# Loads of the scan's factors and stores of its inverses issued by SyncE instead of GpSimd

## The chip, the cores and the metric

The kernel runs on one core of a Trainium2 chip. Engines are named as in the profile: PE (TensorE matmul), PEld (its weight load), DVE (VectorE), ACT (ScalarE), POOL (GpSimd) and SP (SyncE, which computes nothing here and only issues transfers). "SPq", "ACTq" and "POOLq" are rows in which an engine issues a transfer. The metric is the device time of one execution in microseconds (us), as the median of the runs shown.

## What is computed

The reference is the trunk of a diffusion backbone with two layers over 1024 latent tokens and 256 context tokens of width 1024. Layer 0 mixes with pooling and neighbourhood attention, layer 1 with a bidirectional RWKV-7 recurrence; each is followed by a squared-ReLU MLP. The change lies in the recurrence of layer 1:

```
def step(S, inp):
    w_t, k_t, v_t, kk_t, kka_t = inp[:5]
    S = (S * w_t[:, :, None, :]
         - jnp.einsum('bhij,bhj->bhi', S, kk_t)[..., None] * kka_t[:, :, None, :]
         + v_t[..., None] * k_t[:, :, None, :])
    y = jnp.einsum('bhij,bhj->bhi', S, inp[5]) if emit else None
    return S, y
...
for d, reverse in enumerate((False, True)):
    s_ctx, y_c = wkv_scan(s0, decay_c, k_dc, v_c, kk_c, a_c, r_c, reverse)
    _, y_d = wkv_scan(s_ctx, decay, k_d, v, kk, a, r, reverse)
```

16 heads of 64 carry a state of 64 x 64 each, forward and in reverse; the context's final state starts the latent scan.

## The kernel before

All arithmetic is fp32, as products of fp32 matmuls or of split operands. The program runs in stages: layer 0, its MLP, the features of layer 1 (`l1_features`), the scan (`l1_scan`), the readout (`l1_readout`) and the second MLP.

The features stage leaves in DRAM, for each chunk of 64 tokens and each direction, the factors of the scan (`ft`, loaded into tiles `FT`), the strictly lower score blocks (`ls`) and the values (`v1scr`). The scan works through 20 steps, 4 of context (s = 0 to 3) and 16 latent ones (s = 4 to 19), each with two halves, one for each direction d. What a half needs:

- `FT` (L1574, function `load`): the factors of step s and direction d, in one of four fixed tiles, loaded by quarters (two head pairs each) of 256 KB, or 192 KB in the context. The first step's loads are issued by ACT, all others by Pool. `scores` (L1626, tile `sc`) read them one quarter at a time, `stack` (L1608) copies a part, `readout_state` (L1701) reads another part.
- `D` (L1578, `load_values`): the values, on SP.
- `G` and `ZT` (L1594, L1595, `load_blocks`) and `TT` (L1603, `load_inverses`): blocks of `ls` and of the inverses, in many 128-byte rows, on SP. `compose1` (L1653) and `compose2` (L1667) join two 32-row inverses into a 64-row one.
- `chain_x`, `chain_u`, `chain_s` (L1678, L1686, L1729) carry the state `SS` on; `readout_values` (L1713) ends in the copy `yt` (L1717) on ACT and two stores `yscr` (L1720) on SP.

The 32-row inverses come from `scan_blocks` and `scan_invert`. For two steps at a time, eight loads fill `M` from `ls` (L1497, on SP), Pool sets `X` to the identity (L1501, L1502), and DVE does 31 rank-one updates (`tmp` L1511, `X` L1515), then a transposed copy (L1518). `X` and `M` are stored to DRAM as `lt` and `ltt` (L1522, L1523), from which `TT` and `ZT` of two steps are loaded. Ten such blocks are needed. The two first are inverted during the features stage; the other eight run on DVE in the background of the scan, one update at each call of `fill()`, which stands eight times in each half. Early readout work takes their place once they are done.

From step 0 on the order of instructions is the order in which the code is written (`manual_schedule`), engine by engine. In half d of step s stand, in this order among others: the values of step s + 1; `chain_x`; scores of the first quarter of s + 1; quarters 2 and 3 of an FT tile loaded half a step after its quarters 0 and 1; `chain_u`; blocks or `compose1`; `readout_state` and `chain_s`; quarter 0 of FT for step s + 2; `readout_values`; inverses or blocks for s + 2; the last scores; quarter 1 of FT for s + 2. So every quarter is asked for at least half a step before its scores run.

An engine issues its transfers in order, and a transfer that waits holds up all behind it. SP and ACT transfers complete on eight semaphores taken in turn (DMAHW0 to DMAHW7 in the order's rows), Pool's on eight others (DMASW0 to DMASW7); before a transfer is issued, the one that had its semaphore before must have landed. So SP and ACT together have at most eight transfers in flight, and Pool eight more.

Of the kernel before, what the change touches and what calls it, by code (L numbers as in the profile page):

```python
# [58 lines left out]
class Trunk:  # L59
# [1445 lines left out]
    def scan_invert(self, ip, b, M, X):  # L1505

        nc = self.nc
        for c in range(31):
            m, n = c + 1, 31 - c
            tmp = ip.tile([128, 256], F32, tag="tmp", name="tmp", bufs=1)[:, :m * n].rearrange("p (a b) -> p a b", a=m)  # L1510
            nc.vector.tensor_tensor(  # L1511
                out=tmp, in0=X[:, 0:m, c:c + 1].to_broadcast([128, m, n]),
                in1=M[:, c:c + 1, c + 1:32].to_broadcast([128, m, n]), op=ALU.mult,
            )
            nc.vector.tensor_tensor(out=X[:, 0:m, c + 1:32], in0=X[:, 0:m, c + 1:32], in1=tmp, op=ALU.subtract)  # L1515
            yield
        XT = M
        nc.vector.tensor_copy(out=XT, in_=X.rearrange("p r t -> p t r"))  # L1518
        lt = self.scan_dram.tile([128, 32, 32], F32, name=f"lt{b}")
        ltt = self.scan_dram.tile([128, 32, 32], F32, name=f"ltt{b}")  # L1520
        q = nc.sync if b < 2 else nc.gpsimd
        q.dma_start(out=lt, in_=X)  # L1522
        q.dma_start(out=ltt, in_=XT)  # L1523
        self.lt_[b], self.ltt_[b] = lt, ltt

    def l1_scan(self):
        nc, a = self.nc, self.a
        with ExitStack() as es:
# [35 lines left out]
            def load(s, d, parts=range(4)):  # L1564

                if s >= NSTEP:
                    return
                w = W[s]
                F = w["F"][d] = FTs[(2 * s + d) % 4]
                f0 = 0 if w["lat"] else 1  # L1570
                for i in parts:
                    w["got"].add((d, i))
                    hs = slice(2 * i, 2 * i + 2)
                    (nc.scalar if s == 0 else nc.gpsimd).dma_start(out=F[:, hs, 1 + f0:], in_=self.ft[s, d, :, hs, f0:])  # L1574

            def load_values(s, d):
                D_ = hp_.tile([128, 8, 2, CH], F32, tag=f"D{d}", name="D")
# [212 lines left out]
            for d in range(2):  # L1790
                load(0, d)
                load_values(0, d)
                nc.gpsimd.memset(W[0]["D"][d][0:64], 0.0)
# [3 lines left out]
            for d in range(2):  # L1797
                for g in range(4):
                    scores(0, d, g)
                stack(0, d)  # L1800
                load(1, d)
# [10 lines left out]
            for s in range(NSTEP - 1):  # L1812
# [5 lines left out]
                for d in range(2):  # L1818
                    load_values(n, d)
                    chain_x(s, d)  # L1820
                    carry()
                    scores(n, d, 0)
                    load(*later[d], (2,))
                    fill()
                    scores(n, d, 1)
# [31 lines left out]
            s = NSTEP - 1  # L1857
# [392 lines left out]
```

## Time and profile before

| what | us |
|---|---|
| three runs, median (lowest to highest) | 3535.57 (3532.26 to 3536.0) |
| the profiled execution: its own time | 3529.58 |
| the profiled execution: span, first to last instruction | 3527.5 |
| PE busy | 3289.8 (93%) |
| DVE busy | 2049.0 (58%) |
| ACT busy | 1440.4 (41%) |
| POOL busy | 430.9 (12%) |

The span and the 2.1 us around it are the profiled execution's own time. In the table of its DMA queues, q1 is SP's queue (321.55 MB in 405376 packets, 30.9% of the 16 engines' time), q0 is Pool's (81.81 MB in 24640 packets, 7.5%), q10 ACT's (1.77 MB) and q8 and q14 carry instructions. Of the transfers that Pool issues, 152 are FT loads, 8 are lt and 8 ltt stores. The scan lies between about 2190 and 2645 us.

In the lists of waits a row names engine and line, what released it, and the total, the count and the longest wait in us; "issue" as a releaser means that the engine waited for nothing that the profile shows. Timeline rows give start, length, engine, line, operation, output<-input and count, and in brackets the idle time before and its releaser.

### The profile page before, as it was taken

What the parts mean: (1) busy time and instruction counts of PE and PEld (TensorE: products, weight loads), DVE (VectorE), ACT (ScalarE), POOL (GpSimd) and SP (SyncE); (2) the same over time, 40 slices, a digit from 0 to 9 for tenths busy, and PEclk for the clock granted to TensorE, in tenths of its full rate; (3) what the DMA queues carried; (4) which work ended last, traced back from release to release, by engine and by line L of the source; (5) the groups of instructions that cost most, each with busy time, mean ns of one, the idle gap of its engine ahead of it and who ended that gap; (6) DMA issues with size and microseconds to landing.
All of it is one profiled execution on the core that took longest, in us unless ns stands there. A gap on an engine that the chain in (4) does not pass through costs nothing. (4 is left out here: it accounts for less than half of the span.)

```text
span 3527.5 us, 62517 instructions
## 1 busy us (share of the span) xinstructions
PE 3289.8 (93%) x25466; PEld 2747.2 (78%) x25466; DVE 2049.0 (58%) x3903; ACT 1440.4 (41%) x2743; POOL 430.9 (12%) x564
## 2 busy tenths in 40 slices
PE   8999889999999999989988876888888899999998
PEld 4787767888888889867877775777787788888887
DVE  4255555344444354496758988788766734444446
ACT  4244456312121212176758665666664521111112
POOL 0010110000000000023420001232341200000000
PEclk9999999999999999999999898899899899999999
DMA  8433243222222211143227677888873411111112
GB/s 280 149 92 87 91 138 126 96 84 84 75 83 83 78 48 43 36 144 98 77 70 208 213 227 240 174 205 193 224 203 124 156 43 48 48 48 48 48 48 78
DMA packets 432622, 409.11 MB, mean 116 GB/s; under 512 B 151584, under 2 KB 362400, under 8 KB 432336
## 3 DMA queue, kind: packets, MB, share of 16 engines
q1 hardware_dynamic: 405376, 321.55, 30.9%
q0 software_dynamic: 24640, 81.81, 7.5%
q8 instruction: 200, 3.28, 0.4%
q10 hardware_dynamic: 2320, 1.77, 0.2%
q14 instruction: 86, 0.70, 0.1%
HBM read 292.54 MB, written 112.49 MB: 115 GB/s over the span
## 5 line engine op out<-in xcount | busy, mean ns | idle before, releaser
L916 DVE TENSOR_TENSOR yacc<-yps,yacc 128x512 f32<-128x512 f32 x540 | 369.8, 690 | 304.1 <-PE yps L93 303.7
L74 ACT CAST wh<-st 128x1024 fp32r<-128x1024 f32 x160 | 165.0, 1049 | 760.0 <-PE yps L93 557.8
L93 PE MATMUL yps<-wh,xh 128*128 128x512 f32 x1152 | 453.2, 393 | 2.6 <-ACT xh L74 1.5
L93 PE MATMUL yps<-wh,xl 128*128 128x512 f32 x1152 | 448.6, 390 | 0.7 <-DVE xl L75 0.7
L93 PE MATMUL yps<-wl,xh 128*128 128x512 f32 x1152 | 448.9, 390 | 0.0
L75 DVE TENSOR_TENSOR wl<-st,wh 128x1024 fp32r<-128x1024 f32 x160 | 194.3, 1229 | 277.3 <-ACT wh L74 277.1
L93 PE MATMUL acc<-h2h,wh 128*128 128x426 f32 (+3 forms) x768 | 275.6, 359 | 3.1 <-ACT y L671 3.1
L93 PE MATMUL acc<-h2h,wl 128*128 128x426 f32 (+3 forms) x768 | 274.2, 357 | 0.0
L93 PE MATMUL acc<-h2l,wh 128*128 128x426 f32 (+3 forms) x768 | 273.9, 357 | 0.0
L93 PEld LDWEIGHTS yps<-wh,xh 128*128 128x128 f32 x1152 | 216.3, 188 | 70.6 <-DVE yacc L916 11.6
L93 PEld LDWEIGHTS yps<-wh,xl 128*128 128x128 f32 x1152 | 216.1, 188 | 47.8 <-DVE xl L75 2.3
L93 PEld LDWEIGHTS yps<-wl,xh 128*128 128x128 f32 x1152 | 216.3, 188 | 44.8 <-issue 1.7
L898 DVE TENSOR_TENSOR r<-r 128x428 f32<-128x428 f32 (+4 forms) x164 | 102.4, 624 | 243.9 <-ACT r L897 243.8
L93 PE MATMUL acc<-mh,wh 128*128 128x256 f32 (+1 forms) x640 | 215.3, 338 | 4.3 <-ACT mh L74 4.2
L93 PE MATMUL acc<-ml,wh 128*128 128x256 f32 (+1 forms) x640 | 214.4, 335 | 0.0
L93 PE MATMUL acc<-mh,wl 128*128 128x256 f32 (+1 forms) x640 | 214.0, 335 | 0.0
L93 PE MATMUL acc<-h2bh,wh 128*128 128x512 f32 (+3 forms) x544 | 211.9, 389 | 1.4 <-ACT wh L74 0.7
L93 PE MATMUL acc<-h2bl,wh 128*128 128x512 f32 (+3 forms) x544 | 211.8, 389 | 0.8 <-DVE h2bl L288 0.7
L93 PE MATMUL acc<-h2bh,wl 128*128 128x512 f32 (+3 forms) x544 | 211.5, 389 | 0.3 <-DVE wl L75 0.3
L897 ACT ACTIVATE r<-acc 128x428 f32<-128x428 f32 (+4 forms) x164 | 89.2, 544 | 295.1 <-PE acc L93 270.3
L1626 PE MATMUL sc<-FT 64*128 64x192 f32 (+1 forms) x1280 | 144.3, 357 | 16.6 <-issue 6.5
L93 PEld LDWEIGHTS acc<-h2h,wh 128*128 128x128 f32 x768 | 145.0, 189 | 16.1 <-issue 5.1
(322 smaller groups left out, 6996.1 us busy)
## 6 DMA issues: line engine op xcount, KB each, us to landing
st<-in_mlp_w SPq DMA_DIRECT2D x128, 512.0 KB
ft<-F SPq DMA_DIRECT2D x64, 512.0 KB
FT<-ft POOLq DMA_DIRECT2D x128, 256.0 KB, 6.0
adas<-in_ada_w POOLq DMA_DIRECT2D x112, 256.0 KB, 3.8
adas<-in_ada_w SPq DMA_DIRECT2D x80, 256.0 KB
x<-x SPq DMA_DIRECT2D x28, 512.0 KB
bias<-in_bias SPq DMA_DIRECT2D x64, 192.0 KB
ls<-ls SPq DMA_DIRECT2D x80, 128.0 KB
```

Source lines behind the costliest of these rows:

```text
L74: self.nc.scalar.copy(out=hi, in_=src)
L75: self.nc.vector.tensor_tensor(out=lo, in0=src, in1=hi.bitcast(F32), op=ALU.subtract)
L93: self.nc.tensor.matmul(out=ps, lhsT=lhs[x], rhs=rhs[y], start=first and i == 0, stop=last and i == 2)
L897: nc.scalar.activation(out=r, in_=ps, func=AF.Relu)
L898: nc.vector.tensor_tensor(out=r, in0=r, in1=r, op=ALU.mult)
L916: nc.vector.tensor_tensor(out=yacc[t][:, n], in0=ps, in1=yacc[t][:, n], op=ALU.add)
L1626: nc.tensor.matmul(out=p4[:, j, e, f], lhsT=F[st[e], 2 * g + j, 3:5].rearrange("p a t -> p (a t)"), rhs=F[st[e], 2 * g + j, f], start=True ...
```

## The change

Two lines choose another issuing engine. The stores of the inverses b = 2 to 9 (b = 0 and 1 were on SP already) and the loads of the factors for all steps but the first go from `nc.gpsimd` to `nc.sync`. No tile, size or wait condition is written differently.

```
@@ scan_invert
-        q = nc.sync if b < 2 else nc.gpsimd
+        q = nc.sync
         q.dma_start(out=lt, in_=X)
         q.dma_start(out=ltt, in_=XT)
@@ l1_scan, load
-                    (nc.scalar if s == 0 else nc.gpsimd).dma_start(out=F[:, hs, 1 + f0:], in_=self.ft[s, d, :, hs, f0:])
+                    (nc.scalar if s == 0 else nc.sync).dma_start(out=F[:, hs, 1 + f0:], in_=self.ft[s, d, :, hs, f0:])
```

The order of PE, DVE and ACT stays as it was; SP's and Pool's change. On SP at the start of the scan (FT_19564 and FT_19565 are the tiles of step 1, TT_19568 that of step 0) a piece of the difference reads:

```order
 L1595 DMA ZT<-ltt_17783 32x16x32
 L1603 DMA TT_19568<-lt_17782 32x16x32 x2
+L1574 DMA FT_19564<-ft 128x2x192 x4
+L1574 DMA FT_19565<-ft 128x2x192 x4
 L1594 DMA G<-ls 32x16x32
 L1595 DMA ZT<-ltt_17783 32x16x32
```

Eight FT loads, which Pool issued at its own time, now stand behind the last TT of step 0; after them come G, ZT and TT of step 1 (eight loads) and then the eight loads of M for block 2.

On SP in a latent step, with the semaphores that each transfer waits for, the order before is:

```order
L1594 DMA G<-ls 32x16x32 [waits DMAHW7_49,PE_49]
L1595 DMA ZT<-ltt_22925 32x16x32 [waits DMAHW0_49]
L1720 DMA yscr<-yt 64x512 [waits DMAHW1_49,Activation_49]
L1720 DMA yscr<-yt 64x512 [waits DMAHW2_49]
L1594 DMA G<-ls 32x16x32 [waits DMAHW3_49]
L1595 DMA ZT<-ltt_22925 32x16x32 [waits DMAHW4_49]
L1578 DMA D<-v1scr 64x1024 [waits DMAHW5_49]
L1720 DMA yscr<-yt 64x512 [waits DMAHW6_49,Activation_49]
```

From the same G up to the same second pair of yscr, which follows, it now reads:

```order
L1594 DMA G<-ls 32x16x32 [waits DMAHW3_49,PE_49]
L1595 DMA ZT<-ltt_22925 32x16x32 [waits DMAHW4_49]
L1574 DMA FT_19562<-ft 128x2x256 [waits DMAHW5_49,PE_49]
L1720 DMA yscr<-yt 64x512 [waits DMAHW6_49,Activation_49]
L1720 DMA yscr<-yt 64x512 [waits DMAHW7_49]
L1594 DMA G<-ls 32x16x32 [waits DMAHW0_49]
L1595 DMA ZT<-ltt_22925 32x16x32 [waits DMAHW1_49]
L1574 DMA FT_19562<-ft 128x2x256 [waits DMAHW2_49,PE_49]
L1578 DMA D<-v1scr 64x1024 [waits DMAHW3_49]
L1574 DMA FT_19562<-ft 128x2x256 [waits DMAHW4_49,PE_49]
L1574 DMA FT_19562<-ft 128x2x256 [waits DMAHW5_49,PE_49]
L1574 DMA FT_19563<-ft 128x2x256 [waits DMAHW6_49,PE_49]
```

Five FT loads have come in between, each with a wait for PE and in the same turn of eight semaphores as the rest. Pool's order in the scan keeps its memsets and its four early readout products and no transfer but the two D of step 0.

## The prediction

> **What bounds the kernel now.** The page gives the size of the whole and the two data queues. The change touches the scan alone, so I cut its two halves out with the view by stretches.
>
> ```profile
> span 3527.5 us, 62517 instructions
> 2190.00:2314.00 124.00, 100.15 (x2230) 88.59 (x2228) 94.04 (x240) 72.07 (x143) 38.25 (x54) 0.84 0.84 185
> 2314.00:2640.00 326.00, 291.90 (x7238) 259.67 (x7233) 258.91 (x538) 211.82 (x401) 117.40 (x136) 0.94 0.82 208
> ```
>
> The columns are length, busy time of PE, weight load, DVE, ACT and POOL, granted clock, DMA share and GB/s. The scan takes about 450 of 3527.5 us. The 16 DMA engines are busy 82 to 84% of it, and in the long second half PE is busy 291.90 of 326 us, so only 34.1 us of PE idle time are there to be won. What fills them is in the list of PE's waits for that stretch (line, releaser: us in total, times, longest), with PE's share of the scan by steps in the groups of lines:
>
> ```profile
> PE p L1667 <- issue: 6.8, 5, 2.4
> PE yp L1701 <- issue: 4.8, 3, 2.8
> PE sc L1626 <- issue: 4.3, 4, 1.9
> PE yp L1713 <- issue: 2.3, 2, 2.2
> PE xp L1678 <- issue: 1.9, 2, 1.6
> PE p L1653 <- issue: 1.8, 2, 0.9
> PE sp L1729 <- issue: 1.4, 2, 0.9
> PE p L1667 <- DVE SS L1734: 3.4, 3, 1.3
> L1678 PE MATMUL xp<-D,ZQ 128*64 128x64 f32 x928 | 37.1, 238 | 4.6 <-ACT TM L1632 2.7 <-issue 1.9
> ```
>
> No row names a transfer, and the biggest sum, 6.8 + 4.8 + 4.3 + 2.3 + 1.9 + 1.8 + 1.4 = 23.3 us, waits for nothing that the profile shows. 928 matmuls at 64 a step are 14.5 steps in 326 us, 22.5 us a step. The timeline of PE shows where such a gap lies:
>
> ```profile
> 2369.97 1.15 PE L1678 MATMUL xp<-D,ZQ 128*64 128x64 f32 x32 [0.56 <-ACT TM L1632]
> 2371.06 1.57 PE L1626 MATMUL sc<-FT 64*128 64x192 f32 x16
> 2375.83 1.02 PE L1701 MATMUL yp<-SS,FT 64*64 64x64 f32 x26
> 2379.70 0.39 PE L1701 MATMUL yp<-SS,FT 64*64 64x64 f32 x6 [2.84 <-issue]
> 2386.22 0.63 PE L1667 MATMUL p<-TT,G 32*32 32x32 f32 x15 [2.36 <-issue]
> 2386.78 1.98 PE L1678 MATMUL xp<-D,ZQ 128*64 128x64 f32 x32
> 2388.68 2.93 PE L1626 MATMUL sc<-FT 64*128 64x192 f32 x16
> ```
>
> The gap of 2.84 us cuts a group of 32 equal matmuls after the 26th: its inputs were there, so what was late is PE's own instruction stream. After the second gap of 2.36 us the same groups take 1.98 and 2.93 us where they took 1.15 and 1.57: the granted clock has dropped, another 2.2 us. That stream comes by DMA (queue q8 below), over the same engines as the scan's data.
>
> ```profile
> q1 hardware_dynamic: 102952, 36.91, 43.5%
> q0 software_dynamic: 12672, 42.35, 37.2%
> q8 instruction: 67, 1.10, 1.3%
> ```
>
> This is the stretch 2250 to 2640: packets, MB, share of 16 engines. SP's queue q1 moves many small packets (36.91 MB in 102952), Pool's q0 few big ones (42.35 MB in 12672, 3.3 KB each). The change makes q0 empty and gives its bytes to q1.
>
> The first half of the scan is bound otherwise. The chain that ended last runs there through stores of ls, then SP issuing M one by one, then a landing, then DVE without a pause:
>
> ```profile
> 2171.78 9.38 DMA ls<-ls
> 2184.89 3.29 DMA ls<-ls
> 2189.28 6.29 DMA ls<-ls
> 2203.38 1.37 SPq L1497
> 2211.94 1.97 SPq L1497
> 2213.95 2.89 DMA M<-ls
> 2216.96 0.20 DVE tmp L1511
> DVE tmp L1511 <- DMA M<-ls: 6.8, 1, 6.8
> ```
>
> The last row, from the list of waits, is DVE's price for that landing: 6.8 us in which its whole queue stood, the scan's masked copies included.
>
> **The change, part by part.**
>
> *Pool gives up 152 loads of FT and 16 stores of inverses.* Pool's waits in the scan are long, but behind them stands little:
>
> ```profile
> POOL FT L1574 <- ACT TM L1632: 80.7, 12, 13.5
> POOL lt L1522 <- DVE X L1515: 59.4, 6, 18.4
> L1574 POOL DMA_DIRECT2D FT<-ft x152: 724/724/747, 2167.0 to 2624.5; - x152
> L1574 ACTq DMA_DIRECT2D FT<-ft x8: 366/404/1268, 2166.6 to 2180.6; - x8
> PEld sc L1626: 0.3, 1
> DMA to landing us min/median/max: 3.4/6.1/10.0
> ```
>
> Pool saves 152 x 0.724 = 110 us of issuing, worth nothing: Pool is busy 117.40 of 326 us and nobody waits on it in steady state. SP pays about what ACT paid for the same load, 0.40 us. Of the consumers of FT only one matmul waited, 0.3 us: landing after 6.1 us is early enough, since each quarter is asked for at least half a step (11 us) ahead of its scores.
>
> *SP's queue gets them.* A step had on SP 2 D, 2 G, 2 ZT, 4 TT, 4 yscr and, on average, 4 M: 18 issues. It now has 8 FT and one of lt or ltt more: 27, or 0.83 us each in a step of 22.5 us. What one costs on SP now:
>
> ```profile
> 2203.38 11.05 SPq L1497 DMA_DIRECT2D M<-ls  x8
> 2420.20 7.40 SPq L1497 DMA_DIRECT2D M<-ls  x8
> 2431.13 2.17 SPq L1603 DMA_DIRECT2D TT<-lt  x4
> SPq L1720 <- ACT yt L1717: 110.7, 24, 10.4
> ```
>
> Alone, 2.17 / 4 = 0.54 us. In a crowd 7.40 / 8 = 0.93 or 11.05 / 8 = 1.38 us: each waits for the completion of the transfer eight places ahead (the order of SP above), and that one shares the engines with Pool's packets. With Pool silent I take 0.54 to 0.6, the TT row, so 27 x 0.57 = 15.4 us of the 22.5. SP's slack today is 110.7 us of waiting for yt over 16 steps, 6.9 a step, and 15.4 + 6.9 = 22.3 just fits. **Steady issue: 0 us**, covered by that slack and by the half step of lead; if the cover is gone, the price is rival two.
>
> *Waits that SP now takes over.* An FT load waits for the scores, the stack copy or the state readout that free its quarter, an lt store for the end of a DVE inversion (up to 18.4 us, 59.4 in six). Behind them on SP stand TT, D, G, ZT and yscr. They stand behind because the program wrote them later; each is wanted half a step or a step later, and in steady state SP stops at the yt of the same half step anyway. 0 us, with a bound of a few us in the first four steps, where no yscr paces SP.
>
> *The start of the scan.* Before it, ACT and Pool load FT together while the last features are stored:
>
> ```profile
> 2168.53 4.33 POOL L1574 DMA_DIRECT2D FT<-ft  x6
> 2173.49 7.44 ACTq L1574 DMA_DIRECT2D FT<-ft  x4
> 2199.80 5.08 POOL L1574 DMA_DIRECT2D FT<-ft  x7 [7.65 <-ACT ZQ L1608]
> DMA packets 14229, 11.63 MB, mean 291 GB/s; under 512 B 4883, under 2 KB 13459, under 8 KB 14227
> ```
>
> The last row is for 2160 to 2200, when the engines ran full at 291 GB/s. Pool's eight loads there (two, then the six shown) carry 8 x 192 KB = 1.6 MB, and 1.6 MB / 291 GB/s = 5.4 us. They leave this crowd and now stand on SP behind TT, when the ls stores are done: the ls part of the chain (9.38 + 3.29 + 6.29) shortens by up to 5.4. They come ahead of M and push it back by the same 5.4, or by 8 x 0.54 = 4.3. But the seven Pool loads at 2199.80 (1.4 MB, 4.7 us), which ran against M, go behind M in the one queue. M's eight issues fall from 11.05 to 8 x 0.54 = 4.3 at best, 6.7 less; DVE's wait for them is 6.8. So between -5.4 - 6.7 + 4.3 = -7.8 and, if neither crowd clears, +4.3. I take **-6 us**, near the end that the 6.8 us row points to.
>
> *The instruction stream.* With one queue of eight transfers in flight instead of two, a block of instructions should stand behind less. No row shows one queue at this load, so bounds: nothing, or all of 23.3 us plus the slow clock after the longer gaps. The 0.94 of the second half is 0.06 x 326 = 19.6 us of clock; I let half of it hang on these gaps, so -33 at most. A gain beyond zero is what the even spread of gaps while both queues are busy suggests, but the engines stay about as full, since the bytes are the same: I take a quarter of 23.3, **-6 us**. An excess the other way, from SP's packets now coming without pauses, is bounded by the same quarter, +6.
>
> The Trainium skill, page "Runtime: NRT & Kernel Launch", section "Instruction fetch mechanics", says that an engine fetches its program in 16 KiB blocks over its own DMA queue while it runs the last one, and that this is mostly hidden. The gap inside a group of 32 does not agree with "hidden"; by the page this term would be 0 and the time 3529.6 us.
>
> **Sum.** -6 - 6 = -12 us on the profiled execution's 3529.58 us, 3517.6. That execution lies 6.0 us under the median 3535.57 of the three runs, so against the median: **3523.5 us**, its own range 3514 to 3534.
>
> **Rivals.**
>
> *One: nothing moves.* FT was never waited for (0.3 us), so its path is off the chain; at the start the eight loads ahead of M take back what the crowd gives (-5.4 + 5.4); the stream's gaps depend on how full the engines are, which stays. For it: the 0.3 us row and the equal bytes. Against it: the 6.8 us wait of DVE under M's slow issues. 3535.6 us, within 5.
>
> The Trainium skill, "DMA: Bandwidth & Descriptors", section "Issuing engines are not separate DMA queues", gives this rival its rule: the transfers share the same 16 engines whoever issues them, and a second issuer saves only issue time. The small wait on FT agrees with it.
>
> *Two, slower: SP's one queue sets the pace.* Place: any step of the second half; mechanism: 27 issues in order, each waiting for the one eight ahead. It decides from 0.83 us an issue. If they cost what M does at 2420.20, 0.93 us, a step is 27 x 0.93 = 25.1 us, 2.6 more, and 14.5 steps are +38 us: 3573 us; half of it in the steps with M only, 3554. For it: 0.93 and 1.38 are measured, and SP would have no slack over its 6.9 us. Against it: those two were taken against Pool's big packets, which then are gone.
>
> *Three: most of the stream's gaps close.* -6 at the start and -24 of the 33 above: 3505.6 us. For it: the gaps are there only where both queues run. Against it: the engines stay full.
>
> *The change does less than it says* cannot be: SP's order holds all the loads and stores, Pool's none.
>
> **From these to the numbers.** Forecast 0.45, rival one 0.24, two 0.16, three 0.15. A measurement of this kernel tells about 0.2%, 7.1 us, from no change. Faster by more: 0.45 x 0.85 + 0.15 + 0.01 = 0.54; slower by more: 0.16 + 0.02 = 0.18; the rest, 0.28, within. The range reaches from 3503, with rival three in it, to 3550, with the weaker half of rival two; stronger cases of both are left out.
>
> **What would show it.** In the changed profile: q0 nearly empty in the scan and q1 with 1 KB packets in its place; DVE's wait for M under 2 us and the first tmp near 2209 instead of 2216.96; SP's M in groups of eight under 6 us; FT still waited for under 2 us by PE; the sum of "issue" on PE in the second half near 17 us. The prediction is wrong if PE or ACT wait for FT, D or TT by more than 5 us in all (rival two), if M lands no earlier, or if the sum of "issue" grows.

## The result, and the profile after

| | median, us | lowest to highest |
|---|---|---|
| before, six runs beside those of the change | 3533.4 | 3523.63 to 3536.0 |
| the change, six runs | 3512.73 | 3506.29 to 3518.65 |

The ratio is 0.9944, with a 95% interval of 0.9932 to 0.9957: about 20 us less (15 to 24). A second set of six runs of the same changed kernel gave 3512.31 us and a ratio of 0.9956 (0.9943 to 0.9969). In the profiled execution the span is 3504.5 us where it was 3527.5; it was the fastest of its six (3506.29 us), so it shows a little more than the medians.

To see where the time went, all traces are cut at the same four matmuls of PE: the one that stood at 2150 us in the trace of before, and those at 2190, 2314 and 2641.6. The view by stretches then reads, first for before and then for the changed kernel (columns as in the prediction):

```profile
2150.00:2190.00 40.00, 22.21 (x241) 20.00 (x241) 36.71 (x94) 17.44 (x40) 10.03 (x16) 0.71 0.86 270
2314.00:2641.60 327.60, 291.94 (x7239) 259.70 (x7234) 258.91 (x538) 213.34 (x404) 117.40 (x136) 0.94 0.82 209
```

```profile
2145.20:2181.10 35.90, 22.51 (x242) 20.02 (x243) 35.15 (x94) 17.25 (x40) 4.44 (x9) 0.74 0.80 244
2181.10:2307.70 126.60, 101.40 (x2231) 89.39 (x2229) 96.36 (x241) 71.88 (x143) 5.79 (x9) 0.83 0.88 192
2307.70:2620.30 312.60, 285.96 (x7239) 254.54 (x7232) 253.63 (x539) 213.50 (x404) 32.52 (x20) 0.96 0.87 222
```

The end of the features stage gives 40.0 - 35.9 = 4.1 us. The first half of the scan takes them partly back: 126.6 us against 124.0, 2.6 more. The second half is the gain: 312.6 us against 327.6, 15.0 less, of which 6.0 are a shorter busy time of the same matmuls (granted clock 0.96 against 0.94) and 9.0 shorter idle time. The stretch before the scan starts 4.8 us earlier than in before; that comes from stages that the change doesn't touch, and was 1.7 us between the second profiles of the two kernels.

A second profile of each kernel confirms the second half: 326.7 us before (its row stands with the experiments), and for the changed kernel

```profile
2310.40:2624.40 314.00, 284.34 (x7242) 252.89 (x7235) 254.74 (x539) 213.83 (x404) 33.58 (x20) 0.97 0.88 219
```

This is 12.7 us less, of which 3.1 are busy time and 9.6 idle time. So the shorter idle time comes back, and the busy time only by half. Over all three stretches the first pair of profiles gives 491.6 - 475.1 = 16.5 us and the second pair 13.5. The profiles don't place what the medians gain beyond that; single executions of one kernel differ by 12 us (3523.63 to 3536.0).

Pool's queue q0 has lost its load over the whole program and is missing from the second half of the scan, where SP's queue now carries everything:

```profile
q1 hardware_dynamic: 449024, 368.22, 36.0%
q0 software_dynamic: 10560, 35.14, 2.9%
q1 hardware_dynamic: 114788, 68.23, 85.5%
q8 instruction: 57, 0.93, 1.3%
```

The two last rows are those of the second half. What PE waits for there, in the list of waits (line, releaser: us, times, longest):

```profile
PE p L1667 <- DVE SS L1734: 7.6, 5, 2.4
PE p L1667 <- issue: 4.8, 5, 1.5
PE xp L1678 <- ACT TM L1632: 3.1, 4, 1.1
PE up L1686 <- issue: 2.3, 2, 1.5
PE p L1653 <- issue: 2.0, 2, 1.1
PE sc L1626 <- DMA FT<-ft: 1.7, 1, 1.7
PE xp L1678 <- issue: 1.1, 2, 0.8
PE yp L1701 <- issue: 1.1, 2, 0.7
PE sc L1626 <- issue: 0.2, 1, 0.2
```

"issue" is down from 23.3 to 4.8 + 2.3 + 2.0 + 1.1 + 1.1 + 0.2 = 11.5 us, and its longest gap from 2.8 to 1.5 us. DVE's row has grown from 3.4 to 7.6 us, some of the gain given back: PE, early, finds the state `SS` not yet ready (5.8 and 8.3 us in the second profiles). FT is waited for once, 1.7 us. In PE's timeline a gap inside a group of equal matmuls is still there, but short, and the clock stays up behind it (1.15 us for the 32 of `sp`):

```profile
2399.38 0.97 PE L1701 MATMUL yp<-SS,FT 64*64 64x64 f32 x25
2401.04 0.45 PE L1701 MATMUL yp<-SS,FT 64*64 64x64 f32 x7 [0.69 <-issue]
2401.42 1.15 PE L1729 MATMUL sp<-D,TM 128*64 128x64 f32 x32
```

Where such gaps lie can be found by counting PE's instructions in the trace (matmuls, weight loads and those of its sequencer). In before, 18 of the 20 "issue" gaps of the second half lie whole multiples of 256 instructions apart, to within one, and each of the 18 ends 1.3 to 1.7 us after a packet of the instruction queue q8 landed. In the changed kernel it is 13 of 14, 1.2 to 1.9 us after a packet, and in all fourteen profiles of this document together 181 of 207. This shows that PE stands there for the next block of its own program. The blocks are not carried more slowly in before: both kernels have 57 packets of q8 in this half, 16 KB each, and one takes 1.17 and 1.11 us on average in the two profiles of before, 1.14 and 1.20 us in those of the change. What changes is how often a block comes too late.

At the start of the scan the timelines show the ls stores, FT and M on SP, PE's scores of step 0, and DVE's first update:

```profile
2188.38 0.80 SPq L1402 DMA_DIRECT2D ls<-ls  x2
2190.89 4.12 SPq L1574 DMA_DIRECT2D FT<-ft  x8
2201.23 5.27 SPq L1497 DMA_DIRECT2D M<-ls  x8
2188.41 6.19 PE L1626 MATMUL sc<-FT 64*128 64x128 f32 x56 [4.39 <-ACT ls L1400]
2209.69 0.19 DVE L1511 TENSOR_TENSOR tmp<-X,M 128x31 f32<-128x31 f32 x1 [6.84 <-DMA M<-ls]
```

M's eight issues take 5.27 us, where they took 11.05. Yet DVE waits for M as long as before, 6.84 us (in the second profiles 4.7 us before and 7.0 us after). SP's slack, in the list of SP's waits over the whole scan, has shrunk from 110.7 us in 24 waits to:

```profile
SPq L1720 <- ACT yt L1717: 19.3, 12, 2.9
```

### The profile page after: what moved, and what is told of

It is laid out like the page before. It is cut to its first block, busy times and chain, and to the rows that moved or that the text cites. A ratio compares the mean times of both kernels' runs of the same rounds, so it can differ in the third digit from the quotient of the medians.

```text
span 3504.5 us, 62351 instructions
## 1 busy us (share of the span) xinstructions
PE 3280.3 (94%) x25466; PEld 2737.5 (78%) x25466; DVE 2043.3 (58%) x3903; ACT 1439.4 (41%) x2743; POOL 307.6 (9%) x396
## 5 line engine op out<-in xcount | busy, mean ns | idle before, releaser
L93 PEld LDWEIGHTS yps<-wh,xh 128*128 128x128 f32 x1152 | 216.2, 188 | 71.2 <-DVE yacc L916 12.1
L1626 PE MATMUL sc<-FT 64*128 64x192 f32 (+1 forms) x1280 | 144.6, 360 | 11.3 <-DVE ZQ L1641 4.9
```

The costliest lines, as they stand in the source:

```text
L93: self.nc.tensor.matmul(out=ps, lhsT=lhs[x], rhs=rhs[y], start=first and i == 0, stop=last and i == 2)
L1626: nc.tensor.matmul(out=p4[:, j, e, f], lhsT=F[st[e], 2 * g + j, 3:5].rearrange("p a t -> p (a t)"), rhs=F[st[e], 2 * g + j, f], start=True ...
```

## The experiments

All medians stand beside runs of the kernel before on the same chip, whose own medians lie between 3528.6 and 3534.2 us, and the ratio is to those. It can differ by 0.1% from the quotient of the two medians; gains below are taken from the ratio. The two last columns are read from the profile: the second half of the scan, cut at the same matmuls, and PE's sum of "issue" in it.

| kernel | median, us | ratio (95%) | second half, us | "issue", us |
|---|---|---|---|---|
| before | 3533.4 | 1 | 327.6 | 23.3 |
| before, second profile | 3525.45 (one run) | | 326.7 | 25.4 |
| the change | 3512.73 | 0.9944 (0.9932 to 0.9957) | 312.6 | 11.5 |
| the change again | 3512.31 | 0.9956 (0.9943 to 0.9969) | 314.0 | 11.7 |
| FT alone on SP | 3513.86 | 0.9948 (0.993 to 0.9965) | 314.2 | 11.5 |
| stores alone on SP | 3523.9 | 0.9982 (0.9971 to 0.9994) | 322.6 | 20.7 |
| FT of steps 6 to 19 on SP | 3515.71 | 0.9956 (0.9939 to 0.9973) | 317.8 | 11.8 |
| FT of steps 1 to 5 on SP | 3521.61 | 0.997 (0.9959 to 0.9981) | 323.4 | 13.0 |
| FT of one direction on SP | 3518.76 | 0.9973 (0.9962 to 0.9983) | 322.0 | 11.3 |
| FT on ACT | 3555.63 | 1.0063 (1.0047 to 1.0079) | 340.9 | 8.5 |
| G, ZT, TT on Pool | 3529.61 | 0.9988 (0.9976 to 1.0) | 324.3 | 18.5 |
| tiny loads on Pool | 3511.8 | 0.9962 (0.9947 to 0.9977) | 323.7 | 14.6 |
| M ahead of FT | 3508.28 | 0.9928 (0.9912 to 0.9944) | 311.5 | 12.1 |
| M ahead, FT by halves | 3523.74 | 0.9982 (0.9969 to 0.9996) | 328.0 | 17.1 |

### Which of the two edits

The loads without the stores (the diff is against the changed kernel, as in all that follow):

```
-        q = nc.sync
+        q = nc.sync if b < 2 else nc.gpsimd
```

> FT loads on SP as in the changed kernel, the stores of the inverses b = 2 to 9 left on Pool. Theory A (PE's instruction blocks come late while two data queues are busy; Pool's 152 FT loads are that second queue): the whole gain, 15 to 20 us under the kernel before, near 3515 us, and PE's sum of "issue" in the second half of the scan near 11.5 us as in the changed kernel. Theory B (the stores matter: an lt store held Pool up to 18.4 us and FT loads behind it): less than half the gain, over 3524 us.

Measured 3513.86 us, the whole gain, and "issue" at 11.5: as theory A had it. Now the stores without the loads:

```
-  (nc.scalar if s == 0 else nc.sync).dma_start(out=F...
+  (nc.scalar if s == 0 else nc.gpsimd).dma_start(out=F...
```

> The stores of the inverses on SP, FT loads left on Pool. Theory A: 16 of 168 transfers leave Pool, so no change beyond 0.2%: 3530 to 3537 us, the sum of "issue" on PE in the second half over 18 us (23.3 before). Theory B: at least half the gain, under 3524 us.

Measured 3523.9 us. With 0.0018 x 3533 this is 6 us under before (2 to 10): more than theory A's nothing, and by the ratio less than half the gain, though the median lies 0.1 us inside theory B's 3524. "issue" is 20.7, as theory A had it. So 16 stores are worth some us by themselves, but hardly any once the loads have left Pool as well (3513.86 against 3512.73). Why is not settled; in the profile of before, an lt store held Pool up to 18.4 us with FT loads behind it.

### Which half of the scan

```
-  (nc.scalar if s == 0 else nc.sync)
+  (nc.scalar if s == 0 else nc.gpsimd if s < 6 else nc.sync)
```

> FT loads on SP only for steps 6 to 19 (asked for from step 4 on, so in the second half of the scan); steps 1 to 5 stay on Pool; the stores on SP. Theory A: the gain of the second half alone, 12 to 16 us, 3517 to 3521 us, and the sum of "issue" there near 11.5 us. Theory S (the gain hangs on the start, on M landing earlier, and only shows up later): 0 to 4 us.

Measured 3515.71 us: 15 to 16 us by the ratio, at the upper end of theory A's gain, with "issue" at 11.8. The stores are in it, so that some 9 to 10 us are left for the loads of steps 6 to 19. And the other way round:

```
+  (nc.scalar if s == 0 else nc.sync if s < 6 else nc.gpsimd)
```

> FT loads on SP only for steps 1 to 5, later ones on Pool; the stores on SP. Theory A: only what the start gives, 0 to 5 us, 3528 to 3534 us, and the sum of "issue" on PE in the second half near 23 us. Theory S: 12 us or more, under 3522 us. The prediction's term for the start would be 6 us.

Measured 3521.61 us, 10 to 11 us by the ratio, of which the stores alone were worth 6: about 4 for the early loads, with the uncertainty of both ratios. The median is under theory S's 3522 only with the stores' share, and theory A's 3528 to 3534 was missed. Stores, early loads and late loads add up to the whole gain: 6 + 4 + 9.5 = 19.5 us. Its "issue" of 13.0 us contradicts theory A, which wanted 23, while the second half takes 323.4 us, near the 322.6 of the kernel whose FT is all on Pool. One profile's sum of "issue" is thus no sure measure of the second half; its length is the better one.

### Is it chance, and the same kernel again

The kernel before, unchanged:

> The kernel before once more, for a second profile of it. If PE's 23.3 us of "issue" in the second half of the scan are a property of the kernel, they come out between 18 and 28 us again, and that half takes 323 to 328 us; if they are chance, they come out near the 11.5 us of the changed kernel.

```profile
2312.90:2639.60 326.70, 287.43 (x7240) 255.57 (x7235) 259.64 (x539) 213.33 (x404) 117.92 (x136) 0.95 0.82 210
PE p L1667 <- issue: 8.4, 6, 3.9
PE p L1653 <- issue: 3.7, 3, 1.9
PE yp L1701 <- issue: 3.6, 3, 1.8
PE up L1686 <- issue: 3.2, 2, 2.9
```

With four smaller rows (2.3, 1.9, 1.4 and 0.9) "issue" is 25.4 us. The gaps fall on other lines than in the first profile, but their sum and the 326.7 us come back.

> The changed kernel once more, for a second profile and as the measure for the two beside it: 3508 to 3517 us, "issue" on PE in the second half of the scan 9 to 14 us.

Measured 3512.31 us, 11.7 us of "issue" and 314.0 us for the second half.

### Two queues, or Pool's queue

```
+  nc.scalar.dma_start(out=F...          (all steps)
```

> All FT loads issued by ACT: two busy queues again, but both with hardware descriptors and 1 KB packets, on the same eight semaphores, so eight transfers in flight in all. Theory Q (two busy data queues delay PE's instruction blocks, whatever the second one is): "issue" on PE in the second half 18 to 24 us. Theory P (Pool's queue does it: eight more transfers in flight, 4 KB packets): "issue" near 11 us. ACT pays 152 x 0.46 = 70 us of issuing, 3.5 us a step, and stands at loads that wait for PE; with ACT at 66% busy that may cost more than the stalls, so the time decides less than the "issue" sum: 3505 to 3520 us if ACT has the room, 3530 to 3560 if not.

Measured 3555.63 us: ACT doesn't have the room. PE's waits in the second half:

```profile
PE xp L1678 <- DMA D<-v1scr: 18.4, 4, 5.7
PE p L1667 <- DVE SS L1734: 8.5, 6, 3.9
PE p L1667 <- DMA TT<-lt: 5.2, 2, 3.1
PE p L1667 <- issue: 2.5, 3, 1.0
PE xp L1678 <- issue: 2.1, 3, 1.7
PE up L1686 <- issue: 1.5, 3, 0.7
PE p L1653 <- issue: 1.3, 2, 0.9
PE sc L1626 <- issue: 1.1, 2, 0.5
```

Two queues were busy and "issue" was 8.5 us, the lowest of all: theory Q, that any second queue delays the instruction stream, finds no support. The test isn't clean, for PE stood idle for 50 us of this half and so wanted its blocks later. The price lies elsewhere: 23.6 us of waiting for D and TT. SP and ACT share one turn of eight semaphores, so SP's transfers now also depend on loads that ACT issues late. The exchange of roles:

```
-  nc.sync.dma_start(out=dh(w["G"][r]) ...      and ZT, TT
+  (nc.gpsimd if s > 1 else nc.sync).dma_start(out=dh(w["G"][r]) ...
```

> FT and the stores on SP as in the changed kernel, but G, ZT and TT of steps 2 to 19 (144 transfers of 64 KB in 128-byte rows) issued by Pool: two busy queues with the roles exchanged and no byte more. Theory Q: "issue" on PE in the second half back to 17 to 24 us and the time at 3525 us or more. Theory P in the form that big packets do it: near 11 us, and 3507 to 3518 us. SP gets back 8 x 0.55 = 4.4 us a step.

Measured 3529.61 us: nearly all of the gain is gone, though Pool's queue carries only a fifth of what it had in before (6.82 against 33.95 MB in this half).

```profile
q1 hardware_dynamic: 57468, 60.88, 73.6%
q0 software_dynamic: 3328, 6.82, 10.1%
PE p L1668 <- issue: 4.9, 3, 3.1
PE p L1654 <- issue: 4.4, 3, 3.7
PE xp L1679 <- issue: 4.0, 4, 1.6
```

With three smaller rows (2.3, 2.1, 0.8) "issue" is 18.5. Pool's packets are here 6.82 MB / 3328 = 2 KB and not 3.3 KB, so FT's packets are not needed for it; both are larger than those of q1 in the changed kernel, 68.23 MB / 114788 = 0.6 KB. Its first half, 131.6 us, is also 5 us longer than the changed kernel's.

```
-  (nc.scalar if s == 0 else nc.sync)
+  (nc.scalar if s == 0 else nc.gpsimd if d else nc.sync)
```

> FT of direction 0 on SP, of direction 1 on Pool (76 loads each); the stores on SP. If each load in Pool's queue costs its share: half the way between the changed kernel and one with all FT on Pool (3523.9), so 3516 to 3521 us and "issue" of 15 to 19 us. If the mere presence of a second, busy queue of Pool's is what counts: "issue" over 20 us and 3522 us or more.

Measured 3518.76 us, between the two, as a share per load would have it. "issue" is only 11.3, against the expected 15 to 19; instead PE waits 6.5 us for FT in this profile.

```
+  if s >= 6:
+      nc.gpsimd.dma_start(out=tiny[4 * d + i], in_=self.ls[0, d, i, 0, 0:32, 0, 0:16])
```

> The changed kernel with 112 tiny transfers added on Pool, one beside each FT load of steps 6 to 19: 2 KB each, 32 pieces of 64 bytes from ls into a tile that nobody reads. If Pool's way of issuing itself (its descriptors and its queue, whatever they carry) delays PE's stream: "issue" 17 us or more and 3518 us or more. If it is what the transfers carry or how long they stand in the queues: 9 to 14 us and within 4 us of the changed kernel.

Measured 3511.8 us, no change beside the 3512.31 of the changed kernel on the same chip. The profiled execution was the slowest of the six, at 3524.53 us, so its second half and its "issue" in the table are not typical; the verdict rests on the times. In it q0 moved next to nothing in the second half:

```profile
q0 software_dynamic: 3104, 0.20, 0.8%
```

So issuing on Pool, and having its queue at work, costs nothing by itself that these runs can tell (the interval is 5 us either way). It must carry data.

### The start, and fewer issues on SP

`next(bg)`, which issues the eight loads of M, goes ahead of the FT loads of step 1:

```
-  load(1, d)                       (behind the scores of step 0)
...
+  next(bg)
+  for d in range(2):
+      load(1, d)
   for e in range(2):
       load_blocks(1, e)
...
-  next(bg)                         (behind compose2(0))
```

> The changed kernel with the eight loads of M for block 2 issued ahead of the FT loads of step 1 instead of behind them (and behind G, ZT, TT of step 1). By the prediction's term for the start, the FT loads ahead of M cost 4.3 to 5.4 us: DVE's wait for M falls from 6.8 to under 2 us, and the time by 3 to 6 us, to 3507 to 3510 us. The rival: PE then waits for FT or G of step 1 instead, and the time stays within 2 us of 3512.7.

```profile
2194.80 4.27 SPq L1497 DMA_DIRECT2D M<-ls  x8
2199.17 5.45 SPq L1574 DMA_DIRECT2D FT<-ft  x8
2206.38 0.43 DVE L1641 TENSOR_TENSOR ZQ<-sc,masks 64x256 f32<-64x256 f32 x1 [6.96 <-ACT TM L1632]
2206.84 0.19 DVE L1511 TENSOR_TENSOR tmp<-X,M 128x31 f32<-128x31 f32 x1
```

The wait for M is gone: `tmp` follows the masked copy at once, and PE waits for no FT or G of step 1. 3508.28 us, 4.4 under the changed kernel as expected. The intervals of the two ratios (0.9912 to 0.9944, and 0.9932 to 0.9957) overlap, so that step is likely rather than sure. Against the kernel before it is 0.7%, and the best of all versions here. On top of it, FT by halves:

```
-  load(*later[d], (2,)) ... load(*later[d], (3,))
+  load_half(*later[d], 1)                 (at the place of quarter 3)
-  load(s + 2, d, (0,)) ... load(s + 2, d, (1,))
+  load_half(s + 2, d, 0)                  (at the place of quarter 1)
```

> M of block 2 ahead of FT of step 1, as before, and FT from step 2 on loaded by halves (512 KB, at the places of the later quarter) instead of quarters: SP issues 23 transfers a step instead of 27. The prediction put the steady issue on SP at 0 us, covered by its slack. If that holds, fewer issues are worth nothing: within 4 us of the 3508.3 us with quarters, and SP's waiting for yt grows. If SP's queue has become the pace in some steps, it is faster by 4 us or more. If the half loads, asked for later and longer on the way, land too late, PE waits for FT by more than 5 us and it is slower.

Measured 3523.74 us, 15 us slower than with quarters. PE's waits in the second half, and SP's slack, first with halves and then with quarters:

```profile
PE p L1677 <- issue: 13.3, 8, 3.6
PE p L1677 <- DVE SS L1744: 9.5, 6, 2.3
PE sc L1636 <- DMA FT<-ft: 4.8, 3, 2.6
PE xp L1688 <- issue: 2.8, 4, 1.1
PE sc L1636 <- issue: 1.0, 1, 1.0
SPq L1730 <- ACT yt L1727: 50.7, 16, 6.1
```

```profile
SPq L1720 <- ACT yt L1717: 22.3, 10, 2.9
2309.60:2621.10 311.50, 282.24 (x7240) 251.25 (x7232) 254.07 (x539) 212.98 (x403) 33.60 (x20) 0.97 0.90 222
```

SP's slack doubled and bought nothing. Late FT explains 4.8 us, close to the 5 that were named, but more came back as "issue": 17.1 us against 12.1, with a longest gap of 3.6, and the clock fell from 0.97 to 0.94. All of it is in one queue, with the same bytes.

## Why the prediction was right or wrong

The forecast (faster, 3523.5 us, within 3503 to 3550) had the sign; the time came out at 3512.73. Predicted were 12 us, measured 15 to 24.

**Pool's gain, 0 us: right.** What comes after the scan is as long as before (from the last cut to the last instruction 885.9 and 883.7 us in the two profiles of before, 884.2 and 885.9 in those of the change), and no row of PE's waits in the second half names Pool.

**Steady issue on SP, 0 us: right, with almost nothing to spare.** The slack did what it was to do: it fell from 110.7 to 19.3 us, and in the second half PE waits only 1.7 us for FT and not at all for D or TT. The price of an issue was put too low for M: the eight groups of M take 5.2 to 9.48 us, 0.84 us an issue on average and not 0.57 (in before 0.97). Rival two decided from 0.83 us over all issues; M alone reached it. The kernel with FT on ACT showed what its failure looks like: 23.6 us of waiting for D and TT.

**Waits that SP takes over, 0 us: right.** SP stood 12.4 us at lt stores, and PE's list names nothing that stood behind them on SP but one FT.

**The start, -6 us: mis-sized, about -1.** From the matmul at 2150 to the one at 2314 the two profiles of before take 164.0 and 162.0 us, those of the change 162.5 and 161.2. The crowd term was right: the stretch before the scan fell from 40.0 to 35.9 us, -4.1 for a predicted bound of -5.4, and every kernel whose FT of step 1 is on SP shows it (35 to 36 us; 37.6 with one direction there), the others not (39 to 41). M's crowd cleared too, 11.05 to 5.27 us for a predicted 6.7 less. The step that failed is the delay ahead of M, put at 4.3 us. SP's first M now comes 2201.23 - 2188.41 = 12.8 us after the scores of step 0 begin; before it was 2203.38 - 2196.36 = 7.0. These 5.8 us are the 4.12 of the FT issues and slower issues of G, ZT and TT behind them, and they eat the 11.05 - 5.27 = 5.8 that M saves. The second profiles agree: M comes 6.6 us later and is issued 5.4 us faster. DVE's wait stayed at 6.8 us in the first pair, and grew by 2.3 us in the second. What the crowd term gave is also partly lost, since the first half grew by 2.6 us (4.0 in the second pair): in the first pair the scores of step 0 start 1.0 us later after the cut, the first `tmp` another 0.7, and 0.9 us are lost behind it. The forecast that the first `tmp` would stand near 2209 came true (2209.69) because everything before it was earlier, not because M was. Putting M first showed it: that wait fell to nothing, and the stretch from 2150 to 2314 to 159.6 us.

**The instruction stream on PE, -6 us: mis-sized, about -14.** The second half fell from 327.6 and 326.7 us to 312.6 and 314.0. "issue" fell by half (24 to 11.6 us) and not by a quarter, and 6.0 and 3.1 us of busy time came on top. In the first half of the scan it did not fall: 8.9 and 10.9 us before, 8.4 and 10.3 after. What failed is the reason for the quarter, that the engines stay about as full: they were fuller than before (DMA share 0.87 for 0.82) and the gaps still halved. Rival three, at 3505.6 us, had more of this mechanism than the forecast, and the result lies between the two.

**The sum was helped by luck.** The two terms missed by 5 us one way and by 8 us the other, and partly made up for each other. Of the signs that were named, q0 and the wait for FT came as said; "issue" fell further than the 17 us; DVE's wait for M did not fall under 2 us, and M's groups took under 6 us in only three of eight cases. By the sign that M must land earlier, the term for the start was wrong. ACT's one wait for FT, 6.3 us ahead of the scan, was 9.3 us in before and is in neither second profile.

The Trainium skill, "Runtime: NRT & Kernel Launch", section "Instruction fetch mechanics", calls the crossing from one block of instructions to the next mostly hidden. The traces agree in part: in before about two thirds of the crossings show no gap (18 gaps among 57 blocks), but those 18 gaps take 21.6 us of 327.6.

**Why one queue.** Three readings were tried. That any second busy queue delays PE's blocks is not borne out with FT on ACT. That Pool's issuing does so falls with the tiny loads. The third reading fits all but three of the profiles: the blocks come late when more data may stand in the queues at once. Pool's transfers come on top of the eight that SP and ACT may have in flight (before, G/ZT/TT on Pool); ACT's do not; tiny ones hold no data; and halves put more data into SP's eight places. The three that don't fit by "issue" (FT of steps 1 to 5, FT of one direction, and the slow execution with tiny loads) do fit by time. This is argued and not shown: no view counts what stands in the queues ahead of a block, and the halves were also asked for later. A rival that no run excludes is the size of the packets: Pool's were 3.3 and 2 KB in the slow cases, against 1 KB from ACT (27.83 MB in 28872) and 0.6 KB in q1. Only the kernel with halves speaks against it, whose q1 has 0.6 KB packets too.

The Trainium skill, "DMA: Bandwidth & Descriptors", section "Issuing engines are not separate DMA queues", says that a second issuing engine only saves issue time, since all share the same 16 engines. That is why rival one had its chance. The measurements differ from it here: the same transfers took 20 us less of the whole time from SP than from Pool, though no row of PE's waits in the second half of before names one of them. With FT on ACT and the stores on SP it was 22 us more than before; that price, 23.6 us of waiting for D and TT, may be one of issue and order.

## What to carry to other kernels

When PE runs dense code and the DMA engines are as busy as here (82%), look for gaps inside a group of equal matmuls, and count the instructions between them: gaps a multiple of 256 apart were the instruction stream being late. What helped here was one queue with small transfers, not faster issuing. A load that is put ahead of another in one queue delays it by its own issues and by the slowed ones behind it, so order the queue by who is waited for first. Judge such a change by the length of the stretch and by many runs: the sum of one kind of gap in one profile can mislead by 10 us.

## What the runs showed of the hardware

Of 207 "issue" gaps of PE in the second halves of the fourteen profiles, 181 stand whole multiples of 256 of its instructions apart. In the first profiles of before and of the changed kernel these end 1.2 to 1.9 us after a packet of 16 KB landed on the instruction queue.

The same matmuls of the second half do not always take the same busy time. In the first pair of profiles 35.7 us of idle time went with a granted clock of 0.94 and 291.94 us busy, and 26.6 us with 0.96 and 285.96. But the second profile of before had more idle time, 39.3 us, and only 287.43 us busy at 0.95. Over all fourteen profiles the five with under 31 us of idle time were busy for 282 to 287 us, the nine others for 286 to 292. So there is a tendency, and no run shows what a single gap costs in clock.

DVE's busy time for the same 539 instructions there (538 in one trace) was 258.91 and 259.64 us while Pool issued the loads, and 253.63 and 254.74 us without. With the tiny loads on Pool it was 257.3 us, so it goes rather with Pool issuing than with the bytes; the cause wasn't tried.

The time to issue one and the same transfer on SP varies widely: M's eight loads took 4.27 us when they went first and 14.46 us at worst in before, and FT's quarter 0.36 to 1.88 us in the changed kernel.
